# GpSimd's scale and bias products of the first feed-forward norm, planned behind the last row tile's transposes

## The chip, the cores and the metric

The kernel runs on one core of a Trainium2 chip. The time is device time of one execution in microseconds (us), the median of three runs. Every engine takes its instructions from a queue of its own, in the order in which the program put them there, and an instruction waits at the head of its queue until what it needs is there. TensorE (PE in the profile) multiplies matrices into PSUM, VectorE (DVE) and ScalarE (ACT) compute on rows, GpSimd (POOL) computes and issues transfers, SyncE (SP) issues transfers.

## The reference, cut to what matters

x is one sequence of 512 tokens by 1024 features, float32. Two layers follow one another; each has a token mixer and a feed-forward part, each with a residual and a norm behind it:

```python
def layer_norm(x, g, b):
    mu, var = jnp.mean(x, -1), jnp.mean(jnp.square(x - mu), -1)
    return (x - mu) * lax.rsqrt(var + NORM_EPS) * g + b

def conv_ffn(x, w_up, w_conv, w_down):
    h = dwconv_centred(x @ w_up, w_conv)          # three taps along the tokens
    a, g = jnp.split(h, 2, axis=-1)
    return (jax.nn.silu(g) * a) @ w_down          # 1024 -> 2 x 2816 -> 1024

for i in range(DEPTH):                            # layer 0: attention, layer 1: Hyena
    m = mla_mixer(x, ...) if i % 2 == 0 else hyena_mixer(x, ...)
    x = layer_norm(DEEPNORM_ALPHA * x + m, ln1_g[i], ln1_b[i])
    x = layer_norm(DEEPNORM_ALPHA * x + conv_ffn(x, ...), ln2_g[i], ln2_b[i])
```

The Hyena mixer multiplies x by a matrix of 1024 x 3072, passes the result u through three taps along the tokens, and runs two long convolutions one after the other over 1024 channels, as products in the frequency domain, each with a gate:

```python
    for o, gate in enumerate((g1, g2)):
        k_f = jnp.fft.rfft(two_sided_kernel(filt[:, o, 0], filt[:, o, 1]), n=n, axis=0)
        z_f = jnp.fft.rfft(z, n=n, axis=1)
        y = jnp.fft.irfft(z_f * k_f, n=n, axis=1)[:, :length]
        z = gate * (y + d_bias[o] * z)
    return z @ w_o
```

The norm that the change touches is the last line of layer 0, with ln2_g[0] and ln2_b[0].

## The kernel before, in words

The stages run in this order: attention, feed-forward 0, Hyena, feed-forward 1. Each ends with `tail`: a projection back to 1024 features, the residual and the norm. Between stages x lies feature-major (features along the partitions) in two parts, a rounded one (xh) and the rest (xl), so that three matmuls of the fast number format make one exact float32 product (`mm3`, lines 281 to 283: high by high, high by low, low by high). The two parts of anything are made by `split`: ScalarE copies into the high part (line 274), VectorE subtracts (line 276).

The program is written as tasks, Python generators that name ahead of each instruction its engine, a rough cost and the planned time at which its inputs are there. A list scheduler resumes the tasks in the order in which a core would get to them, and each engine's queue is filled in that order. A task can also wait for an event, which another task sets with a planned time, and for room in a pool (`get`, given back by `release` with a planned time). Such a wait is one of the plan: on the chip an instruction waits only for the data and the buffers that it uses. So the plan decides the order in every queue, and nothing else.

`tail` works on four row tiles of 128 tokens. Its second half of columns ends, tile by tile, with the last `dn` matmuls (lines 281 to 283). `norm(t)` then makes one tile: residual from PSUM (line 671), statistics (674, 695, 696), the inverse root (ScalarE at 441, VectorE at 443, 445, 449), and the normalised row (714). It spawns `save(t)` and goes on into `put_x`: two groups of four transposes on TensorE (xTps, line 287), which ScalarE takes out of PSUM with gain and bias as columns (xg, 541), and `split` (274 and 276) for each. So the next stage's x gets its gain and bias on that way.

`save(t)` serves another purpose. It keeps the normalised row in DRAM (xsave) for the residual of the Hyena stage's own `tail`. In this one norm (`rows` holds the gain and the bias as rows; it is empty elsewhere) GpSimd multiplies and adds them, four products of 128 x 512 for a tile, 16 in all (line 733), and then issues the store (735). It works in place on the tile that the transposes read, so it waits for these.

GpSimd's queue also holds the loads of low parts of weights (wlo<-low_117 and so on, line 335) which wait for a buffer in which an earlier piece of weights lies, until the matmuls on that have run.

In the Hyena stage TensorE makes u for 128 channels at a time (lines 281 to 283, accumulators from a pool of six). ScalarE and VectorE apply the taps (1208, 1210, 1212), TensorE transposes the result (utps, 287), and `long_conv` runs on chunks of 256 channels: a forward transform (dft, 1596), some thirty VectorE steps in the frequency domain (all recorded at line 1573: zt, zf, kf), and the transform back (inv, 1655 in the first convolution, 1673 in the second). `long_conv` asks the pool "blk" for six blocks before it is planned; `tail`'s row tiles and rows of gain and bias lie in that pool too, and `save` gives them back.

Of the kernel before, what the change touches and what calls it, by code (L numbers as in the profile page):

```python
# [19 lines left out]
DRAM = bass.MemoryType.DRAM  # L20
# [24 lines left out]
# The program is written as tasks (generators) that name, before each  # L45
# instruction, its engine and rough cost. A small list scheduler resumes them in
# the order in which a core would get to them; each engine's queue gets that order.
# [38 lines left out]
class Pending:  # L86
    """An event that waits for n parts."""
# [12 lines left out]
class Order:  # L100
# [25 lines left out]
    def step(self, task, value):  # L126
        """Resume a task and keep it where its next request is looked for."""
# [16 lines left out]
    def run(self):  # L144
        while True:
# [41 lines left out]
            if r[1] == "PE":  # L187
                # its clock is halved until it has been busy for a while
                if start - self.free.get("PE", -1e9) > COLD:
                    self.cold = COLD  # L190
                if self.cold > 0.0:
                    more = min(cost, self.cold / 2)
                    self.cold -= 2 * more
                    cost += more
# [39 lines left out]
class Trunk:  # L234
# [35 lines left out]
    def split(self, hi, lo, src, n, t, psum=False):  # L270
        """hi, lo: float32r parts of src, exact to the last bits."""
# [17 lines left out]
    def weights(self, src, shape, own=True, low=None, cut=False):  # L289
        """A task that loads a piece of a weight, 4 KB a partition, and splits it; its event.  # L290
        own: in the room for weights, else in two blocks. low: where its low part lies in DRAM, if it does.
        cut: in two transfers."""
# [59 lines left out]
    def low_part(self, src, shape, prio):  # L352
        """A task that puts the low part of a piece of a weight into DRAM ahead of its use; its event."""
# [38 lines left out]
    def columns(self, prio):  # L392
        """The vectors that lie along partitions, one column for each 128 values; their event."""
# [12 lines left out]
    def reduce_angle(self, r, ang, wide, t):  # L406
        """r = ang less the nearest multiple of 2 pi, within [-pi, pi]."""
# [27 lines left out]
    def rsqrt(self, y, m, t):  # L435
        """y = (-2 m) ** -0.5 for a few columns, with one Newton step."""
# [15 lines left out]
    def fm(self, ps, w, n, x, after, halves=False):  # L452
        """ps [P features, S] = sum over k of w(k)^T x(k), float32 in three passes.
        x(k): (hi, lo, event of the first half of the tokens, event of the second)."""
# [22 lines left out]
    def setup(self):  # L477
# [6 lines left out]
        # the array's clock is full only after a few us of work  # L484
# [8 lines left out]
    class X:  # L493
        """Feature-major x in float32r parts: two tiles of 128 features a block."""
# [23 lines left out]
    def put_x(self, x, t, src, times, gain=None):  # L518
        """Token tile t of x from token-major src [P, D]; times: when each half is there.
        gain: event of the columns, and where a gain and a bias to apply on the way lie in them."""  # L520
# [30 lines left out]
    def load_x(self):  # L551
        """The transposed x, laid out as [4, P, 2, S]."""
# [29 lines left out]
    def tail(self, base, lhs, w, nk, g, b, last, free_lhs, late, low=(), beats=()):  # L582
        """x <- LayerNorm(ALPHA x + lhs^T w), token-major; lhs(k): (hi, lo, event).
        late: x is kept without its gain and bias, for the next part to apply. Returns the new x."""
# [23 lines left out]
        norm_ev = Event()  # L608
        go = Event()
# [6 lines left out]
        def loads():  # L616
# [3 lines left out]
            # the table of the square root ahead of the norm  # L620
# [27 lines left out]
        def apply(t, tm, pg):  # L648
            # the gain and the bias of the norm before
# [12 lines left out]
        def residual(t, half, pss, tms):  # L662
            """pss: the accumulators of a half's columns, tms: when they are there."""
# [1178 lines left out]
```

## Time and profile before

| | us |
|---|---|
| median of three runs (lowest, highest) | 1267.77 (1266.93, 1268.64) |
| span of the profiled execution, first to last instruction | 1262.5 |
| TensorE busy | 1238.5 (98%) |
| VectorE busy | 943.5 (75%) |
| ScalarE busy | 568.1 (45%) |
| GpSimd busy | 81.6 (6%) |

The profiled execution's own time is its span and what lies around it; the median is 5.3 us above the span. In the profile a row of the timeline is a run of like instructions on one engine: start, time, engine, line, operation, output and input, shape, how many, and in brackets the idle time just before it and what ended it. The time of an instruction overlaps the next one's a little, so that the price of one in a queue is read from start to start.

### The profile page before, as it was taken

The page shows a single profiled execution, that of the slowest core. Times are in us where ns is not written, and L with a number is a line of the kernel's source. Part 1 is how long each engine was busy: PE and PEld are TensorE (multiplying, and loading weights), DVE is VectorE, ACT ScalarE, POOL GpSimd, SP SyncE. Part 2 cuts the span into 40 slices and gives each one's busy share as a digit, 9 for nine tenths or more (in the row PEclk, how much of TensorE's full clock was granted, in tenths as well). Part 3 has the DMA queues.
Part 4 walks back from the last instruction along what each step waited for, and adds up shares of the span by engine and source line. Part 5 has one row for each costly group of instructions (what it writes and reads, how often), then busy time and mean ns, then how long its engine had stood idle before and what let it go on. Part 6 is the DMA issues. An engine that isn't in the chain of part 4 may idle for free.

```text
span 1262.5 us, 16644 instructions
## 1 busy us (share of the span) xinstructions
PE 1238.5 (98%) x6246; PEld 1051.7 (83%) x6246; DVE 943.5 (75%) x1614; ACT 568.1 (45%) x1086; POOL 81.6 (6%) x140
## 2 busy tenths in 40 slices
PE   8999999999999999999979999999999999999997
PEld 6788888988888888888868888887988888888886
DVE  7898987799997678657677999996566665553626
ACT  5566655644444456534553333232744444433220
POOL 0101000000000001100260000000000000000000
PEclk9999999999999999999989999999999999999999
DMA  5201125543344378999955655456433322323621
GB/s 207 60 28 47 57 70 214 184 136 120 120 143 136 97 261 290 299 350 303 317 194 169 200 170 167 141 190 222 145 100 96 90 98 100 100 89 113 233 67 67
DMA packets 67020, 195.47 MB, mean 155 GB/s; under 512 B 6873, under 2 KB 10713, under 8 KB 66940
## 3 DMA queue, kind: packets, MB, share of 16 engines
q1 hardware_dynamic: 53692, 146.17, 35.4%
q0 software_dynamic: 13248, 48.24, 11.0%
q8 instruction: 49, 0.80, 0.3%
q14 instruction: 31, 0.25, 0.1%
HBM read 160.83 MB, written 33.55 MB: 154 GB/s over the span
## 4 chain that ended last, share of the span: by engine, by line
PE 90%; DVE 4%; DMA 3%; ACT 2%; SPq 0%; issue 0%; DVEq 0%; ACTq 0%
PE up L282 12%; PE up L281 12%; PE up L283 12%; PE dn L281 7%; PE dn L283 7%; PE dn L282 7%; PE u L282 3%; PE u L283 3%; PE u L281 3%; PE dft L1596 2%; PE pTps L287 1%; PE inv L1673 1%; DMA wraw<-in_ffn_w_down_dram 1%; PE inv L1655 1%; ACT xg L541 1%; DVE xl L276 1%
## 5 line engine op out<-in xcount | busy, mean ns | idle before, releaser
L281 PE MATMUL up<-xh,whi 128*128 128x512 f32 (+1 forms) x768 | 286.1, 372 | 0.0
L282 PE MATMUL up<-xl,whi 128*128 128x512 f32 (+1 forms) x768 | 285.5, 372 | 0.0
L283 PE MATMUL up<-xh,wlo 128*128 128x512 f32 (+1 forms) x768 | 285.2, 371 | 0.0
L341 ACT CAST whi<-wraw 128x512 fp32r<-128x512 f32 (+1 forms) x376 | 216.3, 615 | 121.7 <-PE dn L283 94.0
L344 DVE TENSOR_TENSOR wlo<-wraw,whi 128x512 fp32r<-128x512 f32 (+1 forms) x312 | 207.3, 678 | 80.4 <-ACT whi L341 80.1
L283 PEld LDWEIGHTS up<-xh,wlo 128*128 128x128 f32 x768 | 144.6, 188 | 25.1
L281 PEld LDWEIGHTS up<-xh,whi 128*128 128x128 f32 x768 | 144.7, 188 | 24.5
L282 PEld LDWEIGHTS up<-xl,whi 128*128 128x128 f32 x768 | 144.7, 188 | 24.3
L1210 DVE SCALAR_TENSOR_TENSOR cv<-up,cols,cv 128x511 f32<-128x511 f32 x88 | 65.6, 748 | 112.7 <-ACT cv L1208 112.7
L281 PE MATMUL dn<-whi,gated 128*128 128x512 f32 (+1 forms) x374 | 141.4, 378 | 0.1
L282 PE MATMUL dn<-wlo,gated 128*128 128x512 f32 (+1 forms) x374 | 140.9, 377 | 0.0
L283 PE MATMUL dn<-whi,gated 128*128 128x512 f32 (+1 forms) x374 | 140.9, 377 | 0.0
L1208 ACT ACTIVATE cv<-up,cols 128x512 f32<-128x512 f32 x88 | 60.4, 689 | 166.7 <-PE up L283 166.5
L281 PE MATMUL u<-xh,whi 128*128 128x512 f32 (+1 forms) x224 | 87.1, 389 | 0.0
L282 PE MATMUL u<-xl,whi 128*128 128x512 f32 (+1 forms) x224 | 81.5, 364 | 1.6 <-DVE xl L276 1.6
L281 PEld LDWEIGHTS dn<-whi,gated 128*128 128x128 f32 x374 | 70.4, 188 | 13.3 <-DVE xres L671 0.5
L283 PE MATMUL u<-xh,wlo 128*128 128x512 f32 (+1 forms) x224 | 81.3, 363 | 0.0
L283 PEld LDWEIGHTS dn<-whi,gated 128*128 128x128 f32 x374 | 70.4, 188 | 13.0
L282 PEld LDWEIGHTS dn<-wlo,gated 128*128 128x128 f32 x374 | 70.4, 188 | 12.7
L1212 DVE SCALAR_TENSOR_TENSOR cv<-up,cols,cv 128x511 f32<-128x511 f32 x88 | 65.2, 743 | 0.0
L1573 DVE TENSOR_TENSOR zf<-zt 128x512 f32<-128x512 f32 x80 | 51.5, 682 | 0.0
L541 ACT ACTIVATE xg<-xTps,cols 128x128 f32<-128x128 f32 x96 | 38.3, 466 | 27.2 <-PE xTps L287 27.2
(244 smaller groups left out, 2149.7 us busy)
## 6 DMA issues: line engine op xcount, KB each, us to landing
wraw<-in_ffn_up_dram SPq DMA_DIRECT2D x91, 512.0 KB, 3.6
wraw<-in_hy_in_dram SPq DMA_DIRECT2D x46, 512.0 KB, 6.8
wraw<-in_ffn_w_down_dram SPq DMA_DIRECT2D x44, 512.0 KB, 4.5
low<-wlo POOLq DMA_DIRECT2D x32, 512.0 KB, 7.2
wlo<-low POOLq DMA_DIRECT2D x32, 512.0 KB, 3.7
kf<-kfs POOLq DMA_DIRECT2D x16, 512.0 KB, 3.1
kf<-kf SPq DMA_DIRECT2D x16, 512.0 KB, 7.0
wraw<-in_hy_w_o_dram SPq DMA_DIRECT2D x15, 512.0 KB, 6.5
```

Of the source, the lines that this page charges most:

```text
L276: nc.vector.tensor_tensor(lo, src, hi.bitcast(F32), op=ALU.subtract)
L281: mm(ps, lh, rh, start=first, stop=False)
L282: mm(ps, lh, rl, start=False, stop=False)
L283: mm(ps, ll, rh, start=False, stop=last)
L341: nc.scalar.copy(hi[:, s], raw[:, s])
L344: nc.vector.tensor_tensor(lo[:, s], raw[:, s], hi[:, s].bitcast(F32), op=ALU.subtract)
L541: nc.scalar.activation(v[:, j, :], ps[:, j, :], AF.Identity, scale=gb[:, at + d:at + d + 1], bias=gb[:, at + ND + d:at + ND + d + 1])
L1208: nc.scalar.activation(dst, ps, AF.Copy, scale=taps(1))
L1210: nc.vector.scalar_tensor_tensor(dst[:, 1:], ps[:, :S - 1], taps(0), dst[:, 1:], op0=ALU.mult, op1=ALU.add)
L1212: nc.vector.scalar_tensor_tensor(dst[:, :S - 1], ps[:, 1:], taps(2), dst[:, :S - 1], op0=ALU.mult, op1=ALU.add)
L1573: tt = lambda d, a, b, f: nc.vector.tensor_tensor(d, a, b, op=f)
L1596: nc.tensor.matmul(q[:, w], tab[:, r, w], z[:, r], start=True, stop=True)
```

## The change

`tail` gets an event of four parts, `normed`; `norm(t)` sets a part of it when `put_x` has planned the transposes and the split of its tile, and `save(t)` waits for all four before it plans its products and its store. All else in the diff removes comments and docstrings, which moves line numbers (after: 734 and later lines are 5 higher).

```diff
         xres, xev = [None] * NT, [Event() for _ in range(NT)]
         norm_ev = Event()
+        normed = Pending(NT)
         go = Event()
...
-            yield from self.put_x(xnew, t, z, (tm, tm), gcols)
+            normed.done((yield from self.put_x(xnew, t, z, (tm, tm), gcols)))
...
             ts = slice(t * P, (t + 1) * P)
             tp, _ = yield wait(xnew.put[t])
+            if rows:
+
+                td, _ = yield wait(normed.event)
+                tm = max(tm, td)
             for h in range(2 if rows else 0):
                 hs = slice(h * 512, h * 512 + 512)
                 for q, f in zip(lngb, (ALU.mult, ALU.add)):
                     tm = yield op("POOL", pool2(512), tm, tg)
                     nc.gpsimd.tensor_tensor(z[:, hs], z[:, hs], q[:, hs], op=f)
```

Both programs hold the same instructions. Of the queues, VectorE's stays as it was through the whole norm; GpSimd's changes there, and all change in the Hyena stage.

GpSimd's queue in the norm of feed-forward 0, before:

```order
L733 TENSOR_TENSOR xres<-xres,lngb 128x512 x5
L735 DMA xsave_113<-xres 128x1024
L733 TENSOR_TENSOR xres<-xres,lngb 128x512
L335 DMA wlo<-low_117 128x1024
L733 TENSOR_TENSOR xres<-xres,lngb 128x512
L335 DMA wlo<-low_116 128x1024
L733 TENSOR_TENSOR xres<-xres,lngb 128x512 x2
L735 DMA xsave_113<-xres 128x1024
L733 TENSOR_TENSOR xres<-xres,lngb 128x512 x6
L735 DMA xsave_113<-xres 128x1024
L733 TENSOR_TENSOR xres<-xres,lngb 128x512
L335 DMA wlo<-low_120 128x1024
```

and the same stretch of it now, with the lines' new numbers:

```order
L335 DMA wlo<-low_117 128x1024
L335 DMA wlo<-low_116 128x1024
L335 DMA wlo<-low_120 128x1024
L738 TENSOR_TENSOR xres<-xres,lngb 128x512 x8
L740 DMA xsave_113<-xres 128x1024 x2
L738 TENSOR_TENSOR xres<-xres,lngb 128x512 x8
L740 DMA xsave_113<-xres 128x1024 x2
```

The three loads stand ahead of all products. The first eight products are those of row tiles 0 and 1 in turn, the second eight those of 2 and 3. In the built program a product waits for the transposes of its own tile and for the rows of gain and bias, as before; none waits for a later tile.

VectorE in the middle of the Hyena stage (u_7143 and u_7240 are u of one and the same 128 channels in the two programs; a number tells one tile from another), before:

```order
L1573 TENSOR_TENSOR zt_7171<-dft_7182,e2_7186 128x512
L1573 TENSOR_TENSOR kf_7002<-zf_7004,kf_7002 128x1024
L1210 SCALAR_TENSOR_TENSOR u_7143<-u_6908,cols_101,u_7143 128x511
L1573 TENSOR_TENSOR zf_7004<-kf_7002 128x512
L1212 SCALAR_TENSOR_TENSOR u_7143<-u_6908,cols_101,u_7143 128x511
L1573 TENSOR_TENSOR zf_7004<-zt_7006 128x512
```

and now:

```order
L1578 TENSOR_TENSOR zf_7042<-zt_7043,zt_7044 128x512
L1217 SCALAR_TENSOR_TENSOR u2_6975<-u_7017,cols_101,u2_6975 128x511
L1578 TENSOR_TENSOR zf_7042<-zt_7043,zt_7044 128x2x256
L1215 SCALAR_TENSOR_TENSOR u_7240<-u_6974,cols_101,u_7240 128x511
L1215 SCALAR_TENSOR_TENSOR u2_6975<-u_7063,cols_101,u2_6975 128x511
L1578 TENSOR_TENSOR zt_7114<-dft_7345,e2_7352 128x512
L1217 SCALAR_TENSOR_TENSOR u_7240<-u_6974,cols_101,u_7240 128x511
```

Before, u_7143's taps stand among the steps of one convolution whose transform is dft_7100: from the first step on dft_7100 to the second tap of u_7143 there are 33 VectorE instructions, 25 tensor_tensor of 512 columns, 6 of 1024 and 2 scalar_tensor_tensor. Now u_7240's taps stand behind the steps of two convolutions of different chunks (zf_7041, zf_7042 and zf_7059, zf_7060) that alternate: from the first step on dft_7176 to its second tap there are 47, namely 34 of 512, 8 of 1024 and 5 scalar_tensor_tensor. Of these the first 38 (30 and 8) reach to the second step on dft_7203, whose accumulator the matmuls of u_7349 use next.

TensorE at the same place, before:

```order
L1596 MATMUL dft_7270<-u0_6438,dft_6279 128x256 x2
L1596 MATMUL dft_7278<-u0_6438,dft_6279 128x256 x2
L281 MATMUL u_7132<-xh_6166,whi_7090 128x512
L282 MATMUL u_7132<-xl_6167,whi_7090 128x512
L283 MATMUL u_7132<-xh_6166,wlo_7091 128x512
L281 MATMUL u_7132<-xh_6168,whi_7090 128x512
L282 MATMUL u_7132<-xl_6169,whi_7090 128x512
L283 MATMUL u_7132<-xh_6168,wlo_7091 128x512
L287 MATMUL utps_7289<-ident_86,u_7143 128x128 x4
```

and now:

```order
L1601 MATMUL dft_7345<-u0_6399,dft_6276 128x256 x2
L281 MATMUL u_7349<-xh_6162,whi_7221 128x512
L282 MATMUL u_7349<-xl_6163,whi_7221 128x512
L283 MATMUL u_7349<-xh_6162,wlo_7222 128x512
L281 MATMUL u_7349<-xh_6162,whi_7221 128x512
L282 MATMUL u_7349<-xl_6163,whi_7221 128x512
L283 MATMUL u_7349<-xh_6162,wlo_7222 128x512
L281 MATMUL u_7349<-xh_6164,whi_7221 128x512
L282 MATMUL u_7349<-xl_6165,whi_7221 128x512
L283 MATMUL u_7349<-xh_6164,wlo_7222 128x512
L287 MATMUL utps_7365<-ident_86,u_7240 128x128 x4
```

Two rows of `dft ... x2` are what the trace shows as one group x8. Before, from dft_7100 to utps_7289 TensorE has 78 u matmuls, four groups of transforms (two forward, two back) and one of four transposes. Now, from dft_7176 to utps_7365, it has 84 u matmuls and two groups; 75 and the two groups lie ahead of u_7349. Between dft_7150, the transform before, and dft_7176 it has four transposes, six u matmuls and one group, and VectorE has five tensor_tensor of 512 columns between the same two.

## Rows read from the trace of the kernel before

**Rows 1.** The profile's first page: busy time, share of the span and instructions of TensorE and VectorE, and the shares of the chain of work that ended last.

```profile
PE 1238.5 (98%) x6246; PEld 1051.7 (83%) x6246; DVE 943.5 (75%) x1614; ACT 568.1 (45%) x1086; POOL 81.6 (6%) x140
PE 90%; DVE 4%; DMA 3%; ACT 2%; SPq 0%; issue 0%; DVEq 0%; ACTq 0%
```

**Rows 2.** The list of waits of TensorE over the whole span: what waited, for what, us in total, times, the longest.

```profile
PE xTps L287 <- DVE xres L714: 7.1, 1, 7.1
...
PE u L282 <- DVE xl L276: 1.6, 2, 1.1
...
PE dn L281 <- ACT xh L274: 1.2, 1, 1.2
```

**Rows 3.** TensorE's timeline in the norm of feed-forward 0: start, us, line and operation; in brackets the idle time before and what ended it.

```profile
629.64 0.39 PE L282 MATMUL dn<-wlo,gated 128*128 128x512 f32 x1
...
632.37 0.39 PE L282 MATMUL dn<-wlo,gated 128*128 128x512 f32 x1
...
632.83 0.60 PE L287 MATMUL xTps<-ident,xres 128*128 128x128 f32 x4
...
634.41 0.40 PE L283 MATMUL dn<-whi,gated 128*128 128x512 f32 x1
641.91 1.08 PE L287 MATMUL xTps<-ident,xres 128*128 128x128 f32 x4 [7.10 <-DVE xres L714]
...
643.00 0.41 PE L282 MATMUL u<-xl,whi 128*128 128x256 f32 x1
643.22 0.41 PE L283 MATMUL u<-xh,wlo 128*128 128x256 f32 x1
...
648.18 1.03 PE L287 MATMUL xTps<-ident,xres 128*128 128x128 f32 x8
...
653.13 0.39 PE L282 MATMUL u<-xl,whi 128*128 128x256 f32 x1 [0.56 <-DVE xl L276]
...
655.97 0.38 PE L282 MATMUL u<-xl,whi 128*128 128x256 f32 x1 [1.07 <-DVE xl L276]
```

**Rows 4.** Busy time of each engine in stretches of the norm; behind it the granted clock of TensorE (1.00 is full), the share of the DMA engines and what they moved.

```profile
634.00:642.00 8.00, 0.90 (x5) 0.45 (x4) 7.93 (x8) 0.97 (x3) 6.68 (x7) 0.83 0.67 234
642.00:646.00 4.00, 4.00 (x20) 4.00 (x21) 3.20 (x6) 2.79 (x9) 2.90 (x3) 0.50 0.25 97
646.00:650.00 4.00, 4.00 (x35) 4.00 (x35) 3.03 (x8) 3.39 (x10) 1.28 (x2) 0.99 0.61 212
```

**Rows 5.** GpSimd's timeline in the norm.

```profile
628.48 6.77 POOL L733 TENSOR_TENSOR xres<-xres,lngb 128x512 f32<-128x512 f32 x5
...
637.03 0.58 POOL L335 DMA_DIRECT2D wlo<-low  x1
637.63 1.27 POOL L733 TENSOR_TENSOR xres<-xres,lngb 128x512 f32<-128x512 f32 x1
...
656.20 1.30 POOL L733 TENSOR_TENSOR xres<-xres,lngb 128x512 f32<-128x512 f32 x1
```

**Rows 6.** VectorE's timeline in the norm.

```profile
622.77 0.68 DVE L671 SCALAR_TENSOR_TENSOR xres<-xres,dn 128x512 f32<-128x512 f32 x1
...
625.08 0.22 DVE L445 SCALAR_TENSOR_TENSOR nt<-rs,mv 128x1 f32<-128x1 f32 x1
...
625.53 0.81 DVE L714 TENSOR_SCALAR xres<-xres,mv,rs 128x1024 f32<-128x1024 f32 x1
...
627.56 0.95 DVE L276 TENSOR_TENSOR xl<-xg,xh 128x256 fp32r<-128x256 f32 x2
628.47 0.69 DVE L671 SCALAR_TENSOR_TENSOR xres<-xres,dn 128x512 f32<-128x512 f32 x1
...
631.35 4.18 DVE L276 TENSOR_TENSOR xl<-xg,xh 128x256 fp32r<-128x256 f32 x3 [1.04 <-ACT xh L274]
...
635.65 3.29 DVE L445 SCALAR_TENSOR_TENSOR nt<-rs,mv 128x1 f32<-128x1 f32 x1
...
647.05 0.81 DVE L714 TENSOR_SCALAR xres<-xres,mv,rs 128x1024 f32<-128x1024 f32 x1
```

**Rows 7.** Stretches of 20 us in the Hyena stage, columns as in the stretches of the norm.

```profile
700.00:720.00 20.00, 20.00 (x98) 17.18 (x97) 18.77 (x28) 6.95 (x12) 1.07 (x2) 1.00 0.74 252
...
740.00:760.00 20.00, 20.00 (x92) 16.71 (x91) 20.00 (x31) 6.32 (x11) 1.61 (x3) 1.00 0.59 193
```

**Rows 8.** VectorE's timeline in the Hyena stage, at its start and late in it, for the price of one step from start to start.

```profile
669.78 1.29 DVE L1573 TENSOR_TENSOR zt<-dft,e 128x512 f32<-128x512 f32 x2 [4.49 <-PE dft L1596]
...
831.46 4.89 DVE L1573 TENSOR_TENSOR zf<-zt 128x512 f32<-128x512 f32 x8
836.28 0.74 DVE L1210 SCALAR_TENSOR_TENSOR u<-u,cols,u 128x511 f32<-128x511 f32 x1
836.94 1.21 DVE L1573 TENSOR_TENSOR zt<-zf,kf 128x1024 f32<-128x1024 f32 x1
838.07 1.07 DVE L1573 TENSOR_TENSOR u<-inv,u 128x512 f32<-128x512 f32 x1
```

**Rows 9.** Pieces of the chain that ended last, in order of time, at the start of the Hyena stage: start, us, what. The first is one of 15 u matmuls of 512 columns between 662.17 and 665.61.

```profile
662.17 0.23 PE u L281
...
665.61 0.96 PE utps L287 x8
...
667.95 1.73 PE dft L1596 x8
```

## The prediction, made before the changed kernel had run

> **What bounds the kernel now.** I begin with the busy times and the chain that ended last [rows 1]: TensorE is busy for 1238.5 of 1262.5 us and 90% of the chain is its own work. A change can only move the end by opening or closing gaps of TensorE. The list of its waits [rows 2] shows where the gaps are. The largest, 7.1 us, is in the norm of feed-forward 0: the transposes of a row tile wait for VectorE's normalised row (L714). Two waits for a low part xl (L276), 1.6 us together, lie beside it. In the whole Hyena stage there is one gap, 1.2 us at its very end.
>
> TensorE's own rows give the place [rows 3]: the last down matmul starts at 634.41, the transposes of row tile 2 only at 641.91, and two u matmuls are 0.56 and 1.07 us late. After the long gap the granted clock stands at 0.50, the lower of its two levels (1.2 against 2.4 GHz), from 642 to 646, and at 0.99 behind that [rows 4]; 15 matmuls pass 0.213 us apart where the later ones of their shape take 0.12, which is 1.4 us, and the slow transposes add 0.5. So the norm loses 7.1 + 0.56 + 1.07 + 1.4 + 0.5 = 10.6 us. The cause is in the next two groups. GpSimd's products run from 628.48 on, 1.35 us each in a row [rows 5]; VectorE's subtractions of 256 columns, 0.95 us for two at 627.56, take 4.18 us for three beside them, and a three-column step, 0.22 us at 625.08, takes 3.29 [rows 6]. L671, which reads PSUM, takes 0.69 beside a product.
>
> Second, the Hyena stage [rows 7]: in 20 us TensorE is busy for 20.00 and VectorE for 18.77 to 20.00, so these two engines walk in step with nothing to spare, and the order in which each meets the other's results decides.
>
> **The change part by part.** No operation is added or removed: 16 products, 4 stores of xsave, the same matmuls. The wait is one of the planner; in the built program no product waits for row tile 3, only for its own tile, and what moves is queue order.
>
> *GpSimd's queue.* The products move behind three loads of wlo. Each of these waits for a buffer that a down matmul frees, and those start between 629.64 and 632.37 [rows 3]. The last of the three ends at 632.8, its DMA takes about 0.58 us of the queue [rows 5], so the first product starts at about 633.4 instead of 628.48: 5 us later, no more. Then eight run back to back, 10.8 us at 6.77/5 each, with two stores 645.5; the second eight end at 657 (before: 657.5). The loads of wlo go out earlier than before and the stores land some microseconds later, both far ahead of use; I cost them at nothing.
>
> *The norm.* Row tile 2's chain now runs alone: its three subtractions from 631.35 on at 0.48 each, then 1.3 from the three-column step to the end of L714 as row tile 1 took (626.34 - 625.08), with a small step and a fourth subtraction among it, 0.6 more: L714 ends near 634.7 instead of 641.76 and the transposes follow the last down matmul at 634.8 with hardly a gap. But the eight products now lie on row tile 3's chain. VectorE's order there is unchanged: L671, statistics, two subtractions, the three-column step, L714; row tile 1's chain, alone, took 625.53 + 0.81 - 622.77 = 3.6 us [rows 6], and the two subtractions add up to 0.96, so from 634.85 on it would end at 638.4 to 639.4. Three or four of its steps wait for a running product, at 1.0 to 1.35 each, so L714 of row 3 ends at 641.4 to 644.8, in the middle 643.1 (before 647.86). TensorE has 33 u matmuls of 0.119 to do before it needs that row; with the transposes it is through at 639.3, and a new gap of 2 to 5.5 us opens. Row 3's transposes come at about 643.3 instead of 648.18, 4.9 us earlier. Of these I give 1.4 back, for a lower clock behind the new gap and for late subtractions beside the second eight products: **gain 3.5 us**. The bounds are 0 (the gap just moves from one row tile to the next, whole) and 10.6 (no gap is left).
>
> The slowed rows look like a wait for one running product each: 4.18/3 is 1.39 against a product's 1.35 [rows 5, 6]. The Trainium skill, page "SBUF — State Buffer", section "Who interferes with whom", says that a VectorE instruction with two SBUF inputs and a GpSimd instruction that reads SBUF exclude one another, and that the later one blocks until the first has ended. The trace agrees for the three subtractions; for the three-column step it doesn't, which in 3.29 us let two products pass. By the page alone no wait exceeds 1.35 and the upper figure for row 3's L714 falls by up to 1.9 us, the gain rising to some 5.
>
> *The Hyena stage.* The planner now holds the row buffers until the late products, so the first long convolution starts later in its plan, and those of two chunks of channels run in lockstep; the queues differ up to feed-forward 1. I walked down both queues with durations from the trace. VectorE, start to start [rows 8]: 4.82/8 = 0.60 for 512 columns, 1.14 for 1024 (837 to 838 us: 1.13), 0.66 for a scalar_tensor_tensor. TensorE [rows 9]: 3.44/15 = 0.23 for a u matmul of 512 columns, 1.73 for a group of transforms, 0.48 for four transposes.
>
> The place is the first half of one pair of transforms (dft_7176). VectorE is at TensorE's heels there: between dft_7150 and dft_7176 TensorE does 0.48 + 6 x 0.23 + 1.73 = 3.6 us and VectorE 5 x 0.60 = 3.0, so it stands and waits for dft_7176. From there up to the second scalar_tensor_tensor of u_7240 its queue holds 47 instructions: 34 x 0.60 + 8 x 1.14 + 5 x 0.66 = 32.8 us. TensorE, up to the transposes utps_7365 that need u_7240, has 84 u matmuls and two groups: 84 x 0.23 + 2 x 1.73 = 22.8 us. **TensorE stands for 32.8 + 0.1 - 22.8 = 10.1 us** (0.1 from the end of a transform, 667.95 + 1.73, to VectorE's start at 669.78 [rows 8, 9]), most of it one u matmul group earlier, where an accumulator is still held by VectorE's unread transforms. The same sum at the matching place of the order before (dft_7100 to utps_7289): VectorE 25 x 0.60 + 6 x 1.14 + 2 x 0.66 = 23.2, TensorE 78 x 0.23 + 4 x 1.73 + 0.48 = 25.3: no gap, as the trace has none. Behind the new gap VectorE is ahead and the running sums show no further lateness but the 1.2 us of the stage's end, there now too [rows 2]. Bounds: below, 6.4 us, the part that stands already at the accumulator (VectorE's first 38 instructions, 30 x 0.60 + 8 x 1.14 = 27.1, against 75 x 0.23 + 3.46 = 20.7); above, 12.0, if the clock falls behind this gap and costs the 1.9 us that it costs behind the one at 634 us.
>
> **The sum**, against the profiled execution: 1262.5 - 3.5 + 10.1 = 1269.1 us of span. The median before, 1267.77, is 5.3 above that execution's span, so 1274.4.
>
> **The rivals.** *The products leave the norm's chain.* For: row 2's 7.1 us gap is closed with certainty, and if the eight products fall between row 3's instructions its chain is covered too. That page of the Trainium skill, section "Summary: rules for kernel authors", advises just this: of the two engines, schedule the one that is off the critical path. Against: the queue starts them at 633.4, in the middle of row 3's chain. It gives 1262.5 - 10.6 + 10.1 + 5.3 = 1267.3, no change.
>
> *Faster: the lockstep costs nothing.* If VectorE reaches dft_7176 with so much in hand that TensorE never catches the order, only the norm counts: 1262.5 - 3.5 + 5.3 = 1264.3. It needs VectorE's 47 instructions to finish within 22.8 us of the transform; at 0.60 each they can't, unless a part of them had run before. It decides as soon as VectorE is 10 us less loaded than my count.
>
> *Slower still: the gap only moves.* Row 3's chain loses behind eight products what row 2's loses now, with the clock low again; the norm gains 0: 1262.5 + 10.1 + 5.3 = 1277.9. For: the products come closer together than before.
>
> **How the numbers follow.** My forecast 0.69, the products off the chain 0.12, faster 0.08, the gap that only moves 0.11. A measurement of this kernel can tell some 0.2%, 2.5 us, from no change: 1265.2 to 1270.3. The forecast's own spread, gain 0 to 5 and stall 6.4 to 12.0, is about 1270.5 to 1279 and counts as slower; so faster 0.08, same 0.15 (with an edge of the forecast), slower 0.77. The range from 1266.5 to 1280 leaves out the faster case and the tails.
>
> **What would show it.** Right: GpSimd's first product at about 633.4 behind three DMA issues; the 7.1 us wait gone and one of 2 to 5.5 us for L714 ahead of row 3's transposes; a wait of TensorE of 6 to 10 us for VectorE in the middle of the Hyena stage, near 760 us, at a u matmul or at utps, with VectorE busy without a break before it. Wrong: VectorE idle while TensorE waits there, TensorE without a gap from 660 to 855, or products that start after row 3's transposes.

## The result, and the profile after

| | before | after |
|---|---|---|
| median, us (lowest to highest) | 1268.01 (1266.93 to 1268.64) | 1283.05 (1282.41 to 1286.45) |
| ratio of after to before, 95% interval | | 1.0132 (1.0115 to 1.0149) |
| span of the profiled execution | 1262.5 | 1280.5 |
| TensorE, last down matmul of feed-forward 0 to the first utps | 31.03 | 34.24 |
| TensorE, first utps to the first up matmul of feed-forward 1 | 225.86 | 237.88 |

The change costs 15 us, 1.3%. The forecast was slower, 1274.4 us with a range to 1280: right in sign, too small. The last two lines of the table, called the norm and the Hyena stage below, come from the starts of three TensorE instructions. After, these are

```profile
637.29 0.40 PE L283 MATMUL dn<-whi,gated 128*128 128x512 f32 x1
...
671.53 1.12 PE L287 MATMUL utps<-ident,u 128*128 128x128 f32 x8
...
909.41 0.28 PE L281 MATMUL up<-xh,whi 128*128 128x256 f32 x1
```

and before 634.41 [rows 3] and

```profile
665.45 1.12 PE L287 MATMUL utps<-ident,u 128*128 128x128 f32 x8
...
891.31 0.36 PE L281 MATMUL up<-xh,whi 128*128 128x256 f32 x1
```

The stretches hold the whole difference, 3.2 + 12.0 = 15.2 us. The first utps cuts a little differently in the two: after, 132 u matmuls stand ahead of it, before 129. Three of 512 columns, 0.7 us at 0.23 each, have moved from the stage into the norm, so that for equal work the norm loses 2.5 us and the stage 12.7. (The first expectations below have this split, as 2.5 and 12.6.) From the first up matmul to the end of the last down matmul, feed-forward 1 takes the same in both (362.96 and 362.83). Up to the last down matmul of feed-forward 0 the queues of TensorE and VectorE are the same in both programs, and yet it starts at 634.41 in one profile and at 637.29 in the other; in the kernels below it lies between 633.85 and 638.86. So from here on the two stretches are compared and not the spans.

TensorE's list of waits over the whole span, after (what waited, for what, us in total, times, the longest), to be held against [rows 2]:

```profile
PE xTps L287 <- DVE xres L715: 9.3, 1, 9.3
PE u L281 <- DVE zt L1578: 5.0, 1, 5.0
PE dft L1601 <- ACT e L1607: 1.7, 1, 1.7
PE u L282 <- DVE xl L276: 1.6, 2, 1.1
PE utps L287 <- DVE u L1217: 1.5, 1, 1.5
```

The wait in the norm has not gone, it has grown from 7.1 to 9.3 us, and it is still row tile 2's. Three new waits stand in the Hyena stage (zt, e and u), 8.1 us in sum. GpSimd's and VectorE's timelines in the norm show why the first grew ([rows 5] and [rows 6] before). GpSimd:

```profile
635.93 0.54 POOL L335 DMA_DIRECT2D wlo<-low  x1 [0.82 <-PE dn L282]
636.48 9.82 POOL L738 TENSOR_TENSOR xres<-xres,lngb 128x512 f32<-128x512 f32 x8
646.25 1.25 POOL L740 DMA_DIRECT2D xsave<-xres  x2
```

VectorE:

```profile
635.80 0.43 DVE L276 TENSOR_TENSOR xl<-xg,xh 128x256 fp32r<-128x256 f32 x1
636.14 10.71 DVE L715 TENSOR_SCALAR xres<-xres,mv,rs 128x1024 f32<-128x1024 f32 x1
646.77 0.67 DVE L672 SCALAR_TENSOR_TENSOR xres<-xres,dn 128x512 f32<-128x512 f32 x1
```

L715, which takes 0.81 us alone, was asked for at 636.14, 0.34 us ahead of the first product and inside the DMA issue in front of it, and it ended 0.6 us behind the end of the eighth. TensorE's granted clock fell as it did before [rows 4]. In the stretches after, the columns are busy times of PE, PEld, DVE, ACT and POOL, then the granted clock, the DMA share and GB/s:

```profile
637.00:647.00 10.00, 0.69 (x4) 0.24 (x3) 10.00 (x2) 0.84 (x3) 10.00 (x10) 0.74 0.49 182
647.00:651.00 4.00, 4.00 (x19) 4.00 (x20) 3.09 (x10) 2.69 (x8) 1.78 (x2) 0.50 0.65 262
...
766.00:779.00 13.00, 5.80 (x15) 3.95 (x16) 13.00 (x23) 0.71 (x2) 0.00 (x0) 0.58 0.60 203
779.00:783.00 4.00, 4.00 (x24) 3.71 (x22) 3.26 (x6) 0.59 (x1) 0.00 (x0) 0.65 0.00 0
783.00:790.00 7.00, 7.00 (x43) 6.18 (x42) 6.74 (x9) 1.65 (x3) 0.00 (x0) 1.00 0.01 2
```

The last three rows are the place in the Hyena stage: from 766 to 779 VectorE is busy for 13.00 of 13 us and TensorE for 5.80, where before both were full [rows 7]. TensorE's own timeline there:

```profile
766.77 1.13 PE L1601 MATMUL dft<-u,dft 128*128 128x256 f32 x4 [1.68 <-ACT e L1607]
772.85 0.80 PE L281 MATMUL u<-xh,whi 128*128 128x512 f32 x1 [4.95 <-DVE zt L1578]
...
778.54 1.13 PE L287 MATMUL utps<-ident,u 128*128 128x128 f32 x4 [1.48 <-DVE u L1217]
```

### The profile page after: what moved, and what is told of

The parts are those of the page before. It is cut to its first block, busy times and chain, and to the rows that moved or that the text cites. A ratio compares the mean times of both kernels' runs of the same rounds, so it can differ in the third digit from the quotient of the medians.

```text
span 1280.5 us, 16653 instructions
## 1 busy us (share of the span) xinstructions
PE 1245.5 (97%) x6246; PEld 1056.5 (83%) x6246; DVE 946.3 (74%) x1614; ACT 567.6 (44%) x1086; POOL 81.3 (6%) x140
## 5 line engine op out<-in xcount | busy, mean ns | idle before, releaser
L283 PEld LDWEIGHTS dn<-whi,gated 128*128 128x128 f32 x374 | 70.4, 188 | 12.9
L282 PEld LDWEIGHTS dn<-wlo,gated 128*128 128x128 f32 x374 | 70.5, 188 | 12.8
L281 PEld LDWEIGHTS u<-xh,whi 128*128 128x128 f32 x224 | 44.0, 197 | 11.0 <-DVE zt L1578 5.4
```

The source lines that it names most:

```text
L281: mm(ps, lh, rh, start=first, stop=False)
L282: mm(ps, lh, rl, start=False, stop=False)
L283: mm(ps, ll, rh, start=False, stop=last)
```

## The experiments

**Four separations.** The built programs let the parts of the change be taken one by one: every queue of each of these kernels is, row for row, that of before or of after, but for what is named. The cuts of their code leave lines out at each "...".

*Without the products* (a1_no_products):

```diff
                     tm = yield op("POOL", pool2(512), tm, tg)
-                    nc.gpsimd.tensor_tensor(z[:, hs], z[:, hs], q[:, hs], op=f)
+                    pass
```

> The changed kernel without its 16 products (the scale and bias of the residual are left out); every other instruction of every queue stands as in the changed kernel. If the products alone make the norm's loss, the 9.3 us wait ahead of row tile 2's transposes falls below 1 us and the two waits for xl go. If the Hyena stage's loss comes from the order of the queues alone, TensorE's three waits there stay, 8 us in sum and 12.6 with the clock: 1283 - 2.5 - 10.6 = 1270 us. Rival, the loss there comes from the late products or stores: these waits go too, 1257.

Measured 1269.78 us, 1.0027 (1.0015 to 1.0038) of before. From the last down matmul to the first utps it is 21.38 us, 9.7 less than before (10.3 for equal work) and 12.9 less than after; the wait for L715 and those for xl are not in the list. The three waits of the Hyena stage stay to the tenth, and the stage takes 237.77. So the products make the norm's loss, before (where the prediction read 10.6 us) and after, and none of the other.

*The order alone* (a3_order_only): products and stores stand as early as before, and all else as after.

```diff
...
+                    yield op("POOL", 0, tm, tg)
                     nc.gpsimd.tensor_tensor(z[:, hs], z[:, hs], q[:, hs], op=f)
+            if rows:
+                yield op("POOL", 0, tm)
+                nc.gpsimd.dma_start(xsave[ts, :], z)
+                td, _ = yield wait(normed.event)
+                tm = max(tm, td)
+            for _ in range(4 if rows else 0):
+                tm = yield op("POOL", pool2(512), tm, tg)
...
```

> All queues as in the changed kernel, but GpSimd's products stand where their tiles are ready, as early as before the change. Theory 'order': the Hyena stage loses its 12.6 us all the same, the norm is like that before, 1268 + 12.6 = 1280.6 (1278 to 1283). Rival 'late products': the Hyena stage keeps its old time, 1268.

Measured 1276.99 us, 1.0081 (1.0066 to 1.0096). The norm takes 29.78 and the Hyena stage 236.50, with the same three waits (1.7, 5.0, 1.5). The stage loses without the late products; the total is under the expected 1278, since the norm came out 1.3 us better than before, the stage 1.4 better than after, and the kernel before at 1266.89 beside it.

*GpSimd's queue alone* (a4_queue_only): the products are planned at their old places and put into the queue at the new ones, all else is as before.

```diff
...
+            for _ in range(4 if rows else 0):
+                tm = yield op("POOL", pool2(512), tm, tg)
+            t0 = yield op("POOL", 1000, tm)
+            t0 = o.transfer(t0, 512 * 1024)
+            if rows:
+                yield wait(normed.event)
+                kept.append((t, z, lngb))
...
```

> All queues as before the change, but GpSimd's as in the changed kernel. Theory 'order': the norm loses 2.5 us by L714 behind the eight products, and the Hyena stage nothing: 1268 + 2.5 = 1270.5. Rival 'late products': the Hyena stage loses 12.6 here, 1283.

Measured 1267.66 us, 1.0013 (1.0002 to 1.0024); the norm 32.98, the Hyena stage 225.84: the norm loses 1.9 us and the stage nothing. The order is what costs the stage its 12 us. (The time is 1.7 us above the kernel before, at the ratio given, where 2.5 were expected.) In the norm this run held a second case of the long wait, and on another instruction. VectorE's timeline:

```profile
632.70 0.81 DVE L715 TENSOR_SCALAR xres<-xres,mv,rs 128x1024 f32<-128x1024 f32 x1
634.28 0.69 DVE L672 SCALAR_TENSOR_TENSOR xres<-xres,dn 128x512 f32<-128x512 f32 x1 [0.77 <-PE dn L283]
635.00 0.69 DVE L675 BATCH_NORM_STATS2 st<-xres 128x6 f32<-128x512 f32 x1
635.62 9.39 DVE L276 TENSOR_TENSOR xl<-xg,xh 128x256 fp32r<-128x256 f32 x1
```

GpSimd's:

```profile
634.31 0.54 POOL L335 DMA_DIRECT2D wlo<-low  x1 [2.65 <-PE dn L283]
634.87 9.86 POOL L745 TENSOR_TENSOR xres<-xres,lngb 128x512 f32<-128x512 f32 x8
```

Here the loads came a little later against the chain, row tile 2's L715 passed in 0.81 us, and a subtraction of row tile 3's chain waited for the rest of the eight. The statistics just ahead of it (L675, 512 columns out of SBUF) were asked for 0.13 us into the eight products and took the same 0.69 us as in other places: not every instruction that reads SBUF is held off.

*The wait made real* (a10_after_late): all as after, but the products run for row tiles 3 and 2 first, then 1 and 0, so that the first waits on the chip for the last tile's transposes.

```diff
...
+                for pair in (kept[3], kept[2]), (kept[1], kept[0]):
+                    for u, y, qs in pair:
...
```

> The changed kernel with all its queues, only that GpSimd's products stand for row tiles 3 and 2 first and then 1 and 0, so that the first waits on the chip for the last tile's transposes. If the norm's loss and the Hyena stage's are two things that add up, the norm gains what a5_real_late showed (34.2 to 20.3 us from the last down matmul to the first utps), and the Hyena stage keeps its 8 us of waits: 1283 - 13.9 = 1269 (1267 to 1271). Rival: the late products reach into the Hyena stage's order, which has less room than the one before, and it waits for more than 9 us: 1271 or above.

Measured 1268.85 us, 1.0027 (1.0014 to 1.0041); the norm 21.42, the Hyena stage 239.70. The norm gains 12.8 us, the stage has the same three waits (1.7, 5.0, 1.5), so the two parts are separate. They add up to within 2 us: the stage is 1.8 longer than after, and its last 38 us ran at a granted clock of 0.96, where after has 1.00, with no new wait in them. The kernel before took 1265.76 beside it.

**What VectorE waits for.** A small kernel (m1_port): eight products in a row on two tiles by turns, one VectorE instruction behind the first.

```python
nc.gpsimd.tensor_tensor(z, z, rows[:, :512], op=ALU.mult)       # n times
nc.vector.tensor_scalar(col[5], prod[0][:, :1], 1.0, 0.0, op0=ALU.mult, op1=ALU.add)
test()
```

> A small kernel of its own, which computes nothing of the reference: GpSimd runs 8 (or 4) products of 128x512 in a row, and behind the first of them VectorE meets one test instruction, six kinds in turn; in four more segments GpSimd issues a DMA after the fourth product. Theory 'the whole run': an instruction of the form of L715 (tensor_scalar, 1024 columns, one SBUF input) starts only when GpSimd's run has ended: about 7 x 1.25 + 0.8 = 9.5 us behind the first of 8, 3 x 1.25 + 0.8 = 4.5 behind the first of 4; the same instruction with a stride of two, and one that reads PSUM, take what they take alone; a subtraction of two SBUF tiles waits for one product, at most 1.7 in all. Rival 'one product' (the prediction's): L715's form takes at most 1.25 + 0.8 = 2.1 us in every run, and the 10.7 us of the changed kernel have another cause.

The theory of the whole run fell, and so did the hope in a stride. L715's form took 1.67 to 1.88 us in all, also with a stride of two; the subtraction 1.40, the three-column step 1.13, the instruction that reads PSUM 0.68.

The next asked whether it matters what the products depend on (m2_ahead): runs of 4, 8 and 16 on tiles apart, one tile again and again, two and two, in turn.

> A small kernel of its own, nothing of the reference. GpSimd runs one product and then 8 (4, 16) more, VectorE meets one test instruction behind the first: L715's form (1024 columns), a subtraction of two tiles of 256, a three-column step. The runs: eight tiles apart; one tile eight times (each product reads the one before); two and two (multiply, then add on the same tile); two tiles in turn, as the changed kernel has them; 4 and 16 apart. Theory 'ready ahead': where the next products depend on nothing, GpSimd has them in hand before VectorE asks and VectorE waits for the whole run: about 8 x 1.22 = 9.8 us for eight apart, 4.9 for 4, 19.5 for 16; behind one product (1.3 and its own time) where each depends on the one before; behind two at most in two and two; tiles in turn like eight apart. Rival 'one product': at most 1.3 us and the instruction's own time in every run, as in the small kernel before.

The theory 'ready ahead' fell as well: 1.66 or 1.67 us for L715's form (0.99 in the first segment), 1.40 for the subtraction and 1.13 for the three-column step in every run. So the kernel's own long waits held something that the small ones did not. The third varied the point of asking, and put a DMA issue of GpSimd's between the first product and the eight (m3_phase).

> A small kernel of its own, nothing of the reference. As the one before, but VectorE's test instruction is asked for at five points of the product that runs (0 to 1.08 us later, in steps of 0.27), and in twelve more segments while GpSimd issues a DMA, out or in, that eight products follow; eight products of two tiles in turn, as in the changed kernel, against two and two (multiply, add on the same tile). Theory 'the point of asking': an instruction that is asked for early in a product is let in at its end, as in both small kernels so far, and one that is asked for late, or in a DMA issue that products follow, waits through all products that depend on nothing: about 9 to 10 us with tiles in turn, one or two products (1.3 to 2.9 us) with two and two. Rival 'something of the big kernel': never more than one product and the instruction's own time (1.4 to 2.1 us) in any segment; then the waits of 9.4 and 10.7 us have a cause that no small kernel so far has in it.

Without an issue nothing took more than 1.67 us in all, at any point. With one, VectorE's timeline reads (L32 is the subtraction, L29 L715's form; of each the first segment has tiles in turn, the second two and two)

```profile
250.09 10.39 DVE L32 TENSOR_TENSOR half<-half,half 128x256 f32<-128x256 f32 x1
...
262.27 1.74 DVE L32 TENSOR_TENSOR half<-half,half 128x256 f32<-128x256 f32 x1
...
274.71 10.53 DVE L29 TENSOR_SCALAR big<-big,col,col 128x1024 f32<-128x1024 f32 x1
...
287.02 2.01 DVE L29 TENSOR_SCALAR big<-big,col,col 128x1024 f32<-128x1024 f32 x1
```

The three-column step took 10.0 and 1.5, and with a DMA into SBUF instead of out of it all six are the same to 0.12 us. The fourth parts "asked during the issue" from "products behind an issue" (m4_behind).

> A small kernel of its own, nothing of the reference. It parts two readings of the last one: there VectorE waited 10 us when it asked during a DMA issue that products in turn followed. Theory 'behind an issue': products that follow a DMA issue without a pause, and one another, let VectorE in nowhere, also if it asks only in the first or second of them, or if the issue stands in the middle of the run; so with products in turn a subtraction waits to the end of the run in each case behind an issue (9 us when asked in the first product, 7 in the third), not ahead of it; with two and two, or in the mixed run with its first pair behind the issue, at most two products; an instruction that reads PSUM takes 0.7. Rival 'asked during the issue': only what is asked for while the issue runs waits so long, and what is asked for in a product behind it at most 1.3 us and its own time.

GpSimd's issue and run of the second, third and fourth segment, tiles in turn, and of the fifth, two and two:

```profile
28.19 0.60 POOL L57 DMA_DIRECT2D far<-wide  x1
28.81 9.80 POOL L26 TENSOR_TENSOR w<-w,rows 128x512 f32<-128x512 f32 x8
...
40.86 9.80 POOL L26 TENSOR_TENSOR w<-w,rows 128x512 f32<-128x512 f32 x8
...
52.91 9.81 POOL L26 TENSOR_TENSOR w<-w,rows 128x512 f32<-128x512 f32 x8
...
64.97 10.37 POOL L26 TENSOR_TENSOR w<-w,rows 128x512 f32<-128x512 f32 x8
```

and VectorE's subtraction in them:

```profile
29.41 9.48 DVE L32 TENSOR_TENSOR half<-half,half 128x256 f32<-128x256 f32 x1
...
42.24 8.70 DVE L32 TENSOR_TENSOR half<-half,half 128x256 f32<-128x256 f32 x1
...
55.47 7.53 DVE L32 TENSOR_TENSOR half<-half,half 128x256 f32<-128x256 f32 x1
...
65.57 0.97 DVE L32 TENSOR_TENSOR half<-half,half 128x256 f32<-128x256 f32 x1
```

Asked in the first, second or third product behind the issue, it waits to the end of the run; with two and two it waits for one product at most. L715's form does the same: 9.75 and 7.79 us asked in the first and third product behind an issue, 0.63 and 1.09 without one. The rest agrees: asked ahead of the issue it takes 0.42 us, with the issue in the middle of the run 5.96 when asked behind it and 1.12 ahead of it, an instruction that reads PSUM 0.63. Where a single product stood between the issue and the run, it was 9.92 and 8.87: one product does not end the state. In the mixed run, with a pair on one tile first behind the issue and tiles in turn after it, it is 0.82 to 1.17: there the state is over. So what ends it is a place where a product needs the one before it. Such products start 1.34 us apart, others 1.22; whether the dependence itself or this longer step lets VectorE in, no run here parts. One case stands aside: a subtraction asked for 0.34 us into an issue in the middle of a run went through at once, in 0.36, while in m3 one asked for 0.44 us into an issue took 10.39.

*The same in the kernel.* The changed kernel itself holds a run in turn without an issue just ahead of it. Its second eight products stop behind the first of them for the last row tile's transposes, and seven then run in a row:

```profile
654.40 9.50 POOL L738 TENSOR_TENSOR xres<-xres,lngb 128x512 f32<-128x512 f32 x7 [4.95 <-PE xTps L287]
```

VectorE's subtractions beside them take 1.28 us each, about one product's time, and not the whole run:

```profile
657.62 5.13 DVE L276 TENSOR_TENSOR xl<-xg,xh 128x256 fp32r<-128x256 f32 x4 [4.10 <-ACT xh L274]
```

The other way round, with the issue and without the turns, is a6_chained: a4_queue_only with the eight products tile by tile (multiply, add, multiply, add).

```diff
...
-                        for h in range(2):
-                            hs = slice(h * 512, h * 512 + 512)
-                            for k, f in enumerate((ALU.mult, ALU.add)):
-                                for _, y, qs in pair:
+                        for _, y, qs in pair:
+                            for h in range(2):
+                                hs = slice(h * 512, h * 512 + 512)
+                                for k, f in enumerate((ALU.mult, ALU.add)):
...
```

> As a4_queue_only (all queues as before the change, GpSimd's products behind the three loads), but the eight products of two row tiles stand tile by tile (multiply, add, multiply, add) and not in turn. Theory 'ready ahead': VectorE gets in behind one or two products, no wait in the norm is above 4 us, and the stretch from the last down matmul to the first utps is 2 to 5 us shorter than the 32.98 of a4_queue_only: 1263 to 1266. Rival 'any run of eight': the 9.4 us instruction stays, 1267.7.

Measured 1260.65 us, 0.995 (0.9934 to 0.9965) of before. The same sixteen products in another order take 6.7 us off the norm (32.98 to 26.32), more than expected. The eight products still follow an issue:

```profile
638.02 11.74 POOL L745 TENSOR_TENSOR xres<-xres,lngb 128x512 f32<-128x512 f32 x8
```

Up to row tile 3's L715 no VectorE instruction takes more than 1.7 us:

```profile
638.77 0.84 DVE L276 TENSOR_TENSOR xl<-xg,xh 128x256 fp32r<-128x256 f32 x1
...
639.84 1.21 DVE L276 TENSOR_TENSOR xl<-xg,xh 128x256 fp32r<-128x256 f32 x1
...
641.15 1.06 DVE L445 SCALAR_TENSOR_TENSOR nt<-rs,mv 128x1 f32<-128x1 f32 x1
...
642.44 1.65 DVE L715 TENSOR_SCALAR xres<-xres,mv,rs 128x1024 f32<-128x1024 f32 x1
```

**Two versions to beat both.** *Before's order, products really late* (a5_real_late):

```diff
...
+                if len(kept) == NT:
+                    for one in kept[::-1]:
+                        products(*one)
...
```

> All queues as before the change, but GpSimd's products stand in the order of row tiles 3, 2, 1, 0 behind the three loads: the first waits on the chip for the last tile's transposes, so the wait that the change puts into the plan is a real one. With the products out of the chains of row tiles 2 and 3, the 7.1 us gap goes and only late subtractions of tile 3 (L276, two or three us) remain: 1267 - 7 = 1260 (1257 to 1263). Rival, the loss moves to the Hyena stage's first VectorE work or its stores: 1265 or more.

Measured 1256.87 us, 0.992 (0.9903 to 0.9937), just under the expected 1257. TensorE has no wait of 0.1 us left in the norm. GpSimd's first products start at 644.23, behind row tile 3's L715, and its last end at 671.3:

```profile
644.23 3.11 POOL L730 TENSOR_TENSOR xres<-xres,lngb 128x512 f32<-128x512 f32 x2 [4.37 <-ACT whi L341]
```

```profile
642.27 0.81 DVE L715 TENSOR_SCALAR xres<-xres,mv,rs 128x1024 f32<-128x1024 f32 x1
```

The norm takes 20.34 and the Hyena stage 226.53, 0.7 more than before, of which 0.5 is a wait for a late tap.

*No products at all* (a8_late): `tail` of feed-forward 0 called with late, so that VectorE applies gain and bias in the Hyena stage's own tail.

```diff
-                         a["ffn_w_down"][i], NF, a["ln2_g"][i], a["ln2_b"][i], last, free_lhs, False,
+                         a["ffn_w_down"][i], NF, a["ln2_g"][i], a["ln2_b"][i], last, free_lhs, not last,
```

> No products on GpSimd: the gain and bias of this norm are applied by VectorE in the Hyena stage's own tail, as the other norms do it. The norm gains the 9.7 us that a1_no_products showed (31.03 to 21.38 from the last down matmul to the first utps), but the planner makes another order of the Hyena stage: 1258 if it costs nothing, 1270 if it brings the 12 us wait.

Measured 1283.76 us, 1.0129 (1.0108 to 1.015), more than either case expected. The norm takes 23.49, but the planner's other order of the Hyena stage brings waits like those of the changed kernel (2.4, 4.4 and 1.4 us) and one of 10.7 ahead of a late transform back: the stage takes 249.69.

## Why the prediction was wrong

**Right: the queue.** GpSimd's first product came at 636.48, 0.81 us ahead of the last down matmul's start; the prediction's 633.4 was 1.0 ahead of it.

**Right: the stall in the Hyena stage.** The first of VectorE's 47 instructions and the last, the second tap of u_7240, are

```profile
745.58 0.69 DVE L1578 TENSOR_TENSOR zt<-dft,e 128x512 f32<-128x512 f32 x1 [0.50 <-PE dft L1601]
...
777.73 0.75 DVE L1217 SCALAR_TENSOR_TENSOR u<-u,cols 128x511 f32<-128x511 f32 x1
```

VectorE stood 0.50 us for dft_7176, began its steps at 745.58 and ended the second tap of u_7240 at 778.48: 32.9 us for the 47 instructions, predicted 32.8. utps_7365 follows at 778.54. From the transform's end at 745.5 that is 33.0 us for TensorE, 10.2 more than the 22.8 that its work was priced at, predicted 10.1. Two of the three waits are at the accumulator and at utps as forecast; the first, 1.68 us of a transform for a tile of ScalarE's, was not named. As idle time only 8.1 show, since a part of the lateness passes in matmuls at the low clock (0.43 us apart instead of 0.23 from 773 on). Behind the gap the clock is back only at 783, and the stretch as a whole loses 12.0 (12.7 for equal work), about the upper bound that was set for just this. The central value left the clock out, a term at nothing: 1.9 us too little.

**Right size, wrong story: why the order changes.** The prediction had it that the planner holds the row buffers until the late products. It does not: if the products are planned as before and only the blocks are given back up to 25 us later in the plan, every queue stays as it was before. If in the program of before the products cost half or nothing in the plan, the queues of TensorE and VectorE are, row for row, those of after. They are so too if the products stay as they were and only the loads of low parts no longer wait for them in the plan. So it is these loads that count: with the products planned behind them they are planned earlier, the u matmuls come in another order, and two convolutions in lockstep. This was read from the queues of built programs, and not timed by itself.

**Wrong: the norm, and this is the step that failed.** "Row tile 2's chain now runs alone" and "Three or four of its steps wait for a running product, at 1.0 to 1.35 each" gave a gain of 3.5 us where 3.2 were lost (2.5 for equal work). Two things were missed. The chain was not alone: its last instruction was asked for 0.34 us ahead of the first product, while GpSimd issued the DMA in front; the estimate had L714 run from 633.9 to 634.7 with the products starting at 633.4, and did not price that overlap. And the price was not one product but all eight. The 8.6 us between the forecast and the time are 6.7 of the norm and 1.9 of the clock in the stage. With 12.0 and 3.2 in the prediction's own sum it is 1262.5 + 3.2 + 12.0 + 5.3 = 1283.0; measured were 1283.05. That this meets to the tenth is luck: the two profiled spans differ by 18.0 us, 2.9 of them ahead of the norm.

The price of a product was taken from rows in which each second product needed the one before it [rows 5], where VectorE comes in between two. The change put the products of two tiles in turn, behind a DMA issue. The Trainium skill, page "SBUF — State Buffer", section "Who interferes with whom", has the later instruction blocked until the first one ends; these runs agree only without an issue just ahead (m1, m2, the changed kernel's second run) or where each second product needs the one before it (a6). Behind an issue, 7.5 to 10.7 us passed under eight products in turn. The prediction's remark that by the page alone row 3's upper figure falls by 1.9 us does not follow: that figure had no wait above 1.35 in it. One row spoke of it before: the three-column step that took 3.29 us across two products with DMA issues ahead of both [rows 5, 6]. Ahead of the issue and the product in rows 5, GpSimd's timeline has

```profile
635.21 0.59 POOL L735 DMA_DIRECT2D xsave<-xres  x1
635.82 1.27 POOL L733 TENSOR_TENSOR xres<-xres,lngb 128x512 f32<-128x512 f32 x1
```

The prediction noted it as a disagreement and kept the smaller price.

The rival that the gap only moves, priced at 1277.9, was nearest: it put the norm's gain at 0, which was still 3.2 us too good, and had the gap at row tile 3, where it stayed at row tile 2.

**What stays open.** What an issue leaves behind in GpSimd, and why one subtraction inside an issue went through at once, was not tried; nor why L675's statistics passed where a subtraction did not, nor whether other GpSimd instructions than these products hold VectorE off in the same way.

## What to carry to other kernels

Ask of a wait in a planner what it moves in every queue, and sum each moved stretch for the two engines that walk in step: the stall here, though not its clock, could be told from the order and four durations. Where GpSimd works beside a chain of VectorE's, put instructions that depend on one another next to each other, keep DMA issues off the front of long runs, or hold the run back with a real dependence on the chain's last tile: the last gave 1256.87 us, 0.8% under the kernel before. A gain in a gap of TensorE is to be priced with its clock: behind the gaps of 7.1 and 9.3 us the granted clock stood at 0.50 for some 4 us, and behind the waits at 772 us it was back at 1.00 only from 783.

## What the runs showed of the hardware that was not expected

- Behind a DMA issue of GpSimd's own, eight products of 128x512 of two tiles in turn kept three kinds of VectorE instruction out to the end of the run: 7.5 to 10.7 us for a subtraction of two tiles and for a tensor_scalar on one, 10.0 for a three-column step. Without the issue the same run lets them in behind one product (at most 1.9 us in all). Statistics of 512 columns out of SBUF passed beside such a run in 0.69.
- A tensor_scalar on one SBUF tile of 1024 columns waits for a product as the subtraction does (1.67 us in all, 0.63 where it met the end of one), and a stride of two does not free it (1.67 us); a scalar_tensor_tensor with a PSUM input is not held (0.63 to 0.68 us).
- The order of the same eight products, in turn or tile by tile, was worth 6.7 us of the norm (32.98 and 26.32).
